# Three-layer transformer kernel: combination sums read back from DRAM, merging sums on VectorE, gate rows loaded a tile ahead, short head products in other PSUM banks

## The chip, the cores and the metric

The kernel runs on one core of a Trainium2 chip. The time is the device time of one execution in microseconds; less is better. All data are fp32, and each product of two fp32 matrices is made of three passes on TensorE (PE): every operand is split into a high half, rounded to the format that PE reads at full speed (`h` at the end of a name), and the remainder (`l`), and the passes are high by high, high by low and low by high.

## The reference, cut to what matters

Sequence 512, width 2048. Two attention layers, then one hybrid layer with 16 meta tokens in front of the sequence, then a normalization. The change is in the end of the second attention layer and in the hybrid layer:

```python
def hybrid_layer(x, gain, w_in, pool_w, pool_scale, w_attn_up, w_pool_up, w_out):
    h = rmsnorm_2(x, gain)
    zin = h @ w_in
    q, k, v, g_attn, u, g_pool, m_attn, m_pool = jnp.split(zin, cuts, axis=-1)
    o_attn = stick_breaking_attention(q, k, v).reshape(B, L, SB_WIDTH)   # 8 heads of 128
    o_attn = o_attn * jax.nn.silu(g_attn)
    y_attn = o_attn @ w_attn_up
    pooled = multiscale_pool(u)          # mean of the last 2, 4, 8, 16 tokens, minus the token
    mixed = jnp.einsum('blgc,gcd->blgd', pooled, pool_w).reshape(B, L, POOL_WIDTH)
    o_pool = mixed * pool_scale * jax.nn.silu(g_pool)
    y_pool = o_pool @ w_pool_up
    merged = jax.nn.sigmoid(m_attn) * y_attn + jax.nn.sigmoid(m_pool) * y_pool
    return x + merged @ w_out

def stick_breaking_block(q_blk, k_pre, v_pre, q0):
    z = scaled scores of the block with its causal keys
    log_1m_beta = where(causal, log_sigmoid(-z), 0)
    between = cumsum(log_1m_beta, reverse=True) - log_1m_beta
    a = where(causal, exp(log_sigmoid(z) + between), 0)
    return a @ v_pre
```

## The kernel before

Activations stand transposed: a tile holds 128 features by 512 tokens (528 with the meta tokens), and 16 such tiles are the width of 2048. A product of the plain kind takes 24 PE passes of 512 columns per weight tile of 128 by 1024 (eight blocks, three passes each). Other products are done in pairs of token halves and feature halves, as in a fast matrix multiplication with fewer products; for these, `t_set` (line 327) forms combinations of two activation tiles: GpSimd adds the high and low halves of both back together (`ra`, `rb`), VectorE forms four sums of halves (`t12`, `t34`), and these are split again (`t12h`, `t12l`, `t34h`, `t34l`).

Weights come by the queue of SyncE (SP) in the order of use into three buffers (`wr`); ScalarE rounds them to `wh`, VectorE subtracts to get `wl`. Some weights are first summed in DRAM by GpSimd's queue (`wsd`). A load of a weight waits until the `wl` three weights before it is done. All other tiles live in 76 equal slots. PSUM has two groups of four banks: `ps_mm` for the large products and `ps_at` for the heads.

The order of PE's instructions is written out by the program: a main sequence of products (`SEQ2`), and generators beside it that are stepped on a clock of emitted work. `start_side(g, delay)` starts one so many units later, and `yield n` in it waits for n units; a unit is about a nanosecond of PE's work. The orders of the other engines are made by a scheduler. The sequence of the hybrid layer is: projections in pairs (with the four pool products `pw` between them), gate products `gp` and `ga`, `pu` (up projection of the pooled part, into `yp`), `au` (up projection of the attention, merged with `yp` into `mg`), and the output.

Beside it run `t_build` (line 1183), which makes the combinations of the normalized input `X2` during the `gp` products, later those of `mg`; `pool_diff` (line 1165), which forms window mean minus token (`pd`) and splits it for `pw`; and `sb_head` for each of the 8 heads. A head takes `v` to `vt` (transposed, then split into `vh`, `vl`), the scores to `zA`, `zB`, `zC`, a softplus of these on ScalarE (`sp`, split to `sph`, `spl`), sums over blocks on GpSimd (`suf`, split to `sufh`, `sufl`), and then adds to the scores the products with a triangle of ones (`tri`). The short products `zm` and `rm` are the parts of the meta tokens, `so` is the head's output. `vt`, `zm`, `rm` and `so` all take their bank from `ps_at`.

The loads for `pu` (`ol`, the pooled part, line 1199) and for `au` (`sgl`, the gate; `ypl`, the result of `pu`) are issued on ScalarE's queue at the place where the tile is emitted. GpSimd adds `ypl` to the gated product (line 1235) and multiplies all gates (line 445).

Of the kernel before, what the change touches and what calls it, by code (L numbers as in the profile page):

```python
# [18 lines left out]
P = 128  # L19
# [85 lines left out]
def trunk_kernel(ctx, tc, xT, w_in, w_qkv, w_out, w_in2, w_pool, w_aup, w_pup, w_out2, metaT, vec, cst, outT):  # L105
# [9 lines left out]
    def slot(name, dt=F32, cols=S):  # L115
        t = slots.tile([P, W], dt, tag="s", name=name)
        return t[:, :cols]
# [7 lines left out]
    def f32(t):  # L125
        return t.bitcast(F32)
# [200 lines left out]
    def t_set(a, b, rb=None):  # L327


        w = a[0].shape[1]  # L330
        n = w // 2
        lo, hi = slice(0, n), slice(n, w)
        ra = slot("ra", F32, w)
        nc.gpsimd.tensor_tensor(ra, f32(a[0]), f32(a[1]), ALU.add)
        if rb is None:
            rb = slot("rb", F32, w)
            nc.gpsimd.tensor_tensor(rb, f32(b[0]), f32(b[1]), ALU.add)
        t12, t34 = slot("t12", F32, w), slot("t34", F32, w)
        tt(t12[:, lo], ra[:, lo], ra[:, hi], ALU.subtract)
        tt(t34[:, lo], ra[:, hi], rb[:, hi], ALU.subtract)  # L340
        tt(t12[:, hi], rb[:, hi], t12[:, lo], ALU.add)
        tt(t34[:, hi], rb[:, lo], t12[:, hi], ALU.subtract)
        p12, p34 = split(t12, "t12", w), split(t34, "t34", w)

        def cut(p, sl):
            return p[0][:, sl], p[1][:, sl]

        return {"t1": cut(p12, lo), "t2": cut(p12, hi), "t3": cut(p34, lo), "t4": cut(p34, hi),
                "b11": cut(a, lo), "b21": cut(b, lo), "b22": cut(b, hi)}
# [88 lines left out]
    def gate_silu(ps, r, name):  # L438
        g = slot(name + "g")
        tt(g, ps, r, ALU.mult)  # L440
        return silu(g, name)

    def silu(g, name):
        a = gate_sigmoid(g, name)
        nc.gpsimd.tensor_tensor(g, g, a, ALU.mult)
        return g
# [14 lines left out]

    xd = [tc.dram_tile([P, NC, S], F32, name=f"xd{i}") for i in range(2)]
# [325 lines left out]
    def layer(lay, h, rd, x_src, x_dst):  # L788
# [68 lines left out]
        for j in range(NC):  # L857
# [11 lines left out]
            else:  # L869
# [5 lines left out]
                lo = slot("Xl", F32R, W)  # L875
                nc.scalar.mul(real(hi), halves(xg), g2)
# [118 lines left out]
    def sb_head(hd):  # L995
# [51 lines left out]
        pm = ps_at("zm")  # L1047
# [19 lines left out]
        pm = ps_at("rm")  # L1067
# [11 lines left out]
        o = ps_at("so")  # L1079
# [13 lines left out]
    def v_split(vf):  # L1093
        tp = ps_at("vt")
        for j in range(NB):
            transp(tp[:, j * P:(j + 1) * P], vf[:, token(j):token(j) + P])
        return split(tp, "v")
# [5 lines left out]
    gad = tc.dram_tile([P, SB, S], F32, name="gad")  # L1103
    gpd = tc.dram_tile([P, 8, S], F32, name="gpd")
# [60 lines left out]
    def pool_diff(cur, uf, w, res, i):  # L1165
        yield 15000
        d = slot("pd")
        ins = nc.vector.scalar_tensor_tensor(d, cur[:, NM:], 1.0 / w, uf[:, NM:], ALU.mult, ALU.subtract)
        behind_pe(ins)
        res[i] = split(d, "pd")  # L1170
# [12 lines left out]
    def t_build(get, upto):  # L1183
        while len(tset) < upto:
            n = len(tset)
            tset.append(t_set(get(n), get(n + 8)))
            yield 8000
# [7 lines left out]

    def o_load(c):
        op[c] = split(load(opd[:, c, :], "ol", queue=nc.scalar), f"o{c}")

    start_side(t_build(x2, 8), 9000)
    for kind, i in SEQ2:  # L1200
# [25 lines left out]
        elif kind == "au":  # L1226
# [4 lines left out]
            ga = load(sgd[:, i, :], "sgl", queue=nc.scalar)  # L1231
            yp = load(ypd[:, i, :], "ypl", queue=nc.scalar)
            ya = slot("ym")
            tt(ya, run_gemm(1, 8, lambda c: oa[c]), ga, ALU.mult)
            nc.gpsimd.tensor_tensor(ya, ya, yp, ALU.add)  # L1235
            mg[i] = split(ya, f"mg{i}")
            if 8 <= i < 8 + EARLYT:
                tset.append(t_set(mg[i - 8], mg[i], ya))
        elif kind == "gp" and i < GPLAIN:
# [3 lines left out]
            nc.gpsimd.dma_start(gpd[:, i, :], gate_silu(ps, sr, "gp"))  # L1243
# [61 lines left out]
    start_side(t_build(mget, 8))  # L1305
# [165 lines left out]
```

## Time and profile before

| | |
|---|---|
| median of 3 runs | 2718.32 us (2716.43 to 2720.26) |
| profiled execution | 2721.86 us |
| its span | 2720.1 us |
| mean granted clock of TensorE | 0.986 |
| PE busy | 97% |
| DVE (VectorE), ACT (ScalarE), POOL (GpSimd) busy | 67%, 48%, 22% |

The span is the time from the first to the last instruction of the profiled execution; a start or a duration below is in microseconds from its beginning. An engine's busy time leaves out the issuing of transfers. The granted clock is the share of TensorE's full speed (2.4 GHz) that it was given; the lower of its two levels is half of that. A wait is put down to the instruction that released it last.

### The profile page before, as it was taken

The numbers are of one execution on the slowest core, as the hardware profiler recorded it, in microseconds if no ns is written. First come the engines' busy times: TensorE is split into PE (matmuls) and PEld (weight loads), VectorE is DVE, ScalarE is ACT, GpSimd is POOL, SyncE is SP. The second block draws the span as 40 slices with busy tenths as digits, with TensorE's granted clock in tenths as the row PEclk, the third lists the DMA queues.
The fourth block names the chain that finished last, engine by engine and source line by source line (L and its number), as shares of the span: only waits on it lengthen the run. The fifth ranks groups of instructions, "written<-read, shape, count | busy, mean of one in ns | idle before, by whom it ended". The sixth has DMA issues, their size and how long they took to land.

```text
span 2720.1 us, 39186 instructions
## 1 busy us (share of the span) xinstructions
PE 2640.2 (97%) x15169; PEld 2301.7 (85%) x15169; DVE 1832.6 (67%) x2675; ACT 1311.0 (48%) x2160; POOL 601.4 (22%) x553
## 2 busy tenths in 40 slices
PE   8999999999999999999999999999999997999897
PEld 6888888888788888888888899999999986777697
DVE  7767566644476756665587777768777664764787
ACT  5445455532344545553344333336666664632353
POOL 4111132222121113224442122000000131313312
PEclk9999999999999999999999999999999998999999
DMA  5455555577654545457733544555555534364455
GB/s 177 118 142 134 133 138 131 150 223 210 177 147 127 138 128 140 127 162 218 196 108 112 156 152 153 161 157 156 161 157 160 168 128 148 118 218 149 126 184 186
DMA packets 138266, 419.76 MB, mean 154 GB/s; under 512 B 15696, under 2 KB 20176, under 8 KB 138080
## 3 DMA queue, kind: packets, MB, share of 16 engines
q1 hardware_dynamic: 93344, 288.40, 33.6%
q0 software_dynamic: 27312, 97.20, 15.9%
q10 hardware_dynamic: 17424, 31.66, 3.5%
q8 instruction: 119, 1.95, 0.3%
q14 instruction: 67, 0.55, 0.1%
HBM read 375.12 MB, written 119.67 MB: 182 GB/s over the span
## 4 chain that ended last, share of the span: by engine, by line
PE 84%; DVE 6%; DMA 4%; issue 2%; ACT 2%; POOL 2%; SPq 0%; DVEq 0%; ACTq 0%; POOLq 0%
PE mm L160 45%; PE y L160 11%; PE z L160 8%; PE x L160 8%; DMA sgl<-sgd 2%; DVE wl L129 2%; PE msc L160 1%; POOL ym L1235 1%; PE qn L160 1%; PE sc L160 1%; PE mo L160 1%; PE o L160 1%; PE tp L164 1%; PE kn L160 1%; DMA ol<-opd 1%
## 5 line engine op out<-in xcount | busy, mean ns | idle before, releaser
L249 ACT CAST wh<-wr 128x1024 fp32r<-128x1024 f32 (+2 forms) x448 | 461.8, 1031 | 647.6 <-PE mm L160 327.3
L129 DVE TENSOR_TENSOR wl<-wr,wh 128x1024 fp32r<-128x1024 f32 (+2 forms) x448 | 575.6, 1288 | 241.1 <-ACT wh L249 227.5
L160 PE MATMUL mm<-hh,wh 128*128 128x512 f32 x1024 | 411.0, 401 | 6.6 <-ACT wh L249 6.4
L160 PE MATMUL mm<-hh,wl 128*128 128x512 f32 x1024 | 405.1, 396 | 4.3 <-DVE wl L129 4.2
L160 PE MATMUL mm<-hl,wh 128*128 128x512 f32 x1024 | 404.9, 395 | 2.9 <-DVE hl L132 2.9
L227 POOL DMA_DIRECT2D wsd<-in_w_in x128 | 88.3, 690 | 730.9 <-PE mm L160 498.0
L160 PEld LDWEIGHTS mm<-hh,wl 128*128 128x128 f32 x1024 | 193.4, 189 | 50.5 <-DVE wl L129 5.8
L160 PEld LDWEIGHTS mm<-hh,wh 128*128 128x128 f32 x1024 | 193.9, 189 | 42.5 <-ACT wh L249 6.4
L160 PEld LDWEIGHTS mm<-hl,wh 128*128 128x128 f32 x1024 | 193.8, 189 | 40.5 <-DVE hl L132 5.3
L249 ACT CAST wh<-ws 128x1024 fp32r<-128x1024 f32 x111 | 116.4, 1049 | 160.1 <-PE y L160 99.3
L160 PE MATMUL y<-t34h,wl 128*128 128x256 f32 (+1 forms) x592 | 166.9, 282 | 0.0
L160 PE MATMUL y<-t34h,wh 128*128 128x256 f32 (+1 forms) x592 | 166.9, 282 | 0.0
L160 PE MATMUL y<-t34l,wh 128*128 128x256 f32 (+1 forms) x592 | 166.8, 282 | 0.0
L129 DVE TENSOR_TENSOR wl<-ws,wh 128x1024 fp32r<-128x1024 f32 x111 | 138.9, 1251 | 29.0 <-ACT wh L249 26.8
L160 PE MATMUL x<-Xl,wh 128*128 128x256 f32 (+1 forms) x512 | 144.7, 283 | 0.0
L160 PE MATMUL x<-Xh,wl 128*128 128x256 f32 (+1 forms) x512 | 144.5, 282 | 0.0
L160 PE MATMUL x<-Xh,wh 128*128 128x256 f32 (+1 forms) x512 | 144.3, 282 | 0.0
L160 PEld LDWEIGHTS y<-t34h,wl 128*128 128x128 f32 x592 | 111.5, 188 | 0.0
L160 PEld LDWEIGHTS y<-t34h,wh 128*128 128x128 f32 x592 | 111.5, 188 | 0.0
L160 PEld LDWEIGHTS y<-t34l,wh 128*128 128x128 f32 x592 | 111.3, 188 | 0.0
L160 PE MATMUL mm<-Xh,wl 128*128 128x512 f32 x256 | 102.5, 400 | 3.7 <-DVE wl L129 3.7
L160 PE MATMUL mm<-Xh,wh 128*128 128x512 f32 x256 | 103.2, 403 | 0.0
(1036 smaller groups left out, 7170.5 us busy)
## 6 DMA issues: line engine op xcount, KB each, us to landing
wr<-in_w_in SPq DMA_DIRECT2D x256, 512.0 KB, 3.7
wsd<-in_w_in POOLq DMA_DIRECT2D x128, 512.0 KB, 5.3
wr<-in_w_out SPq DMA_DIRECT2D x95, 512.0 KB, 4.5
ws<-wsd SPq DMA_DIRECT2D x37, 512.0 KB, 4.2
wr<-wsd SPq DMA_DIRECT2D x37, 512.0 KB, 4.1
wsd<-in_w_out POOLq DMA_DIRECT2D x20, 512.0 KB, 5.7
xd<-xn SPq DMA_DIRECT2D x32, 256.0 KB, 3.6
sgd<-sga ACTq DMA_DIRECT2D x32, 256.0 KB, 2.2
```

What stands on the lines that cost most here:

```text
L129: nc.vector.tensor_tensor(out, a, b, op)
L160: last_pe[0] = nc.tensor.matmul(out, a, b, start=start, stop=stop, skip_group_check=True).ins
L164: nc.tensor.transpose(out, x, ident)
L227: behind_pe(nc.gpsimd.dma_start(dst, src, **kw))
L249: nc.scalar.copy(hi, raw)
L1235: nc.gpsimd.tensor_tensor(ya, ya, yp, ALU.add)
```

## The change

- At the end of layer 1, each normalized tile is also written, unsplit, to DRAM (`xrd`). `t_set` takes `ra` and `rb` as arguments, and `t_build` loads them (`tr`) on SP's queue one step ahead, so that GpSimd's sums go away. Its first delay goes from 9000 to 6000 units with a yield of 3000 after the first loads.
- The merged tiles are written to DRAM (`mgd`) on ScalarE's queue, except the four whose combinations are made at once; `t_build` and the four early `t_set` read them back.
- The gate products of `gp` and the sums of `au` go from GpSimd to VectorE. Those of `ga` stay.
- `vt`, `zm`, `rm` and `so` take their banks from `ps_mm`.
- `pool_diff` starts 9000 units after its window sums in place of 15000.
- `sgl` and `ypl` for `au` are loaded on SP's queue, issued one tile ahead; `ol` is loaded on SP's queue. The `sgl` of `pu` stays on ScalarE's.

```diff
-    def t_set(a, b, rb=None):
+    def t_set(a, b, ra, rb):
...
-        ra = slot("ra", F32, w)
-        nc.gpsimd.tensor_tensor(ra, f32(a[0]), f32(a[1]), ALU.add)
-        if rb is None:
-            rb = slot("rb", F32, w)
-            nc.gpsimd.tensor_tensor(rb, f32(b[0]), f32(b[1]), ALU.add)
...
-    def silu(g, name):
+    def silu(g, name, eng=nc.gpsimd):
         a = gate_sigmoid(g, name)
-        nc.gpsimd.tensor_tensor(g, g, a, ALU.mult)
+        eng.tensor_tensor(g, g, a, ALU.mult)
...
+                xr = slot("xr", F32, W)
+                nc.scalar.mul(real(xr), halves(xg), g2)
+                nc.scalar.mul(halves(xr)[:, :, :M2], halves(metas[:, j * NM:(j + 1) * NM]), g2)
+                nc.scalar.dma_start(xrd[:, j, :], xr)
...
-        pm = ps_at("zm")
+        pm = ps_mm("zm")
...
-        pm = ps_at("rm")
+        pm = ps_mm("rm")
...
-        o = ps_at("so")
+        o = ps_mm("so")
...
-        tp = ps_at("vt")
+        tp = ps_mm("vt")
...
     def pool_diff(cur, uf, w, res, i):
-        yield 15000
+        yield 9000
...
-    def t_build(get, upto):
-        while len(tset) < upto:
+    def t_build(get, raw, w):
+
+        ahead = {}
+
+        def fetch(n):
+            if n < 8:
+                ahead[n] = [load(raw[:, c, :], "tr", w) for c in (n, n + 8)]
+
+        fetch(len(tset))
+        yield 3000
+        while len(tset) < 8:
             n = len(tset)
-            tset.append(t_set(get(n), get(n + 8)))
+            fetch(n + 1)
+            tset.append(t_set(get(n), get(n + 8), *ahead.pop(n)))
             yield 8000
...
+    def au_loads(i):
+        return load(sgd[:, i, :], "sgl"), load(ypd[:, i, :], "ypl")
+
     def o_load(c):
-        op[c] = split(load(opd[:, c, :], "ol", queue=nc.scalar), f"o{c}")
-
-    start_side(t_build(x2, 8), 9000)
+        op[c] = split(load(opd[:, c, :], "ol"), f"o{c}")
+
+    start_side(t_build(x2, xrd, W), 6000)
...
-            ga = load(sgd[:, i, :], "sgl", queue=nc.scalar)
-            yp = load(ypd[:, i, :], "ypl", queue=nc.scalar)
+                ahead = {0: au_loads(0)}
+            if i + 1 < NC:
+                ahead[i + 1] = au_loads(i + 1)
+            ga, yp = ahead.pop(i)
             ya = slot("ym")
             tt(ya, run_gemm(1, 8, lambda c: oa[c]), ga, ALU.mult)
-            nc.gpsimd.tensor_tensor(ya, ya, yp, ALU.add)
+            tt(ya, ya, yp, ALU.add)
+            if i not in range(8, 8 + EARLYT):
+                nc.scalar.dma_start(mgd[:, i, :], ya)
             mg[i] = split(ya, f"mg{i}")
             if 8 <= i < 8 + EARLYT:
-                tset.append(t_set(mg[i - 8], mg[i], ya))
+                tset.append(t_set(mg[i - 8], mg[i], load(mgd[:, i - 8, :], "tr"), ya))
...
-            nc.gpsimd.dma_start(gpd[:, i, :], gate_silu(ps, sr, "gp"))
+            nc.gpsimd.dma_start(gpd[:, i, :], gate_silu(ps, sr, "gp", nc.vector))
...
-    start_side(t_build(mget, 8))
+    start_side(t_build(mget, mgd, S))
```

The order of PE's instructions is the same in both kernels, row by row. On the other engines it moves. VectorE's order around the third pool product, where `pd` and `pdl` are the two differences and their low halves, `ab` and `c` are sums of the paired products, and `ws` is the sum of two weights; before:

```order
L129 TENSOR_TENSOR ab<-y,m_13817 128x264
L129 TENSOR_TENSOR wl<-wr,wh 128x512
L1168 SCALAR_TENSOR_TENSOR pd<-pl,uf 128x512
L129 TENSOR_TENSOR wl<-ws,wh 128x1024
L129 TENSOR_TENSOR pdl<-pd,pdh 128x512
L1168 SCALAR_TENSOR_TENSOR pd<-pl,uf 128x512
L129 TENSOR_TENSOR ws<-ws,wr 128x1024
L129 TENSOR_TENSOR wl<-wr,wh 128x1024
L129 TENSOR_TENSOR pdl<-pd,pdh 128x512
```

and after:

```order
L129 TENSOR_TENSOR ab<-m_13883,y 128x264
L129 TENSOR_TENSOR wl<-ws,wh 128x1024
L1169 SCALAR_TENSOR_TENSOR pd<-pl,uf 128x512
L129 TENSOR_TENSOR pdl<-pd,pdh 128x512
L1169 SCALAR_TENSOR_TENSOR pd<-pl,uf 128x512
L129 TENSOR_TENSOR wl<-wr,wh 128x1024
L129 TENSOR_TENSOR pdl<-pd,pdh 128x512
L129 TENSOR_TENSOR ab<-y,m_13883 128x264
L129 TENSOR_TENSOR wl<-wr,wh 128x512
```

Both pairs stand ahead of the sum `ab` of `y` and of the 512-column weight (that of `pw` itself), where before they stood behind these.

ScalarE's order at the first head that starts in the last gate tile, where `o0h` to `o3h` are the high halves of the pooled part, `gaa` belongs to the gate and `sp` is the head's softplus; before:

```order
L151 CAST o0h<-ol 128x512
L136 ACTIVATE gaa<-gaa 128x512
L1180 DMA ol<-opd 128x512
L249 CAST wh<-wr 128x1024
L151 CAST o1h<-ol 128x512
L1180 DMA ol<-opd 128x512
L151 CAST o2h<-ol 128x512
L1180 DMA ol<-opd 128x512
L151 CAST o3h<-ol 128x512
L151 CAST vh<-vt 128x512
L136 ACTIVATE sp<-zA 128x512
```

and after:

```order
L151 CAST o0h<-ol 128x512
L136 ACTIVATE gaa<-gaa 128x512
L151 CAST o1h<-ol 128x512
L249 CAST wh<-wr 128x1024
L151 CAST o2h<-ol 128x512
L249 CAST wh<-wr 128x1024
L151 CAST o3h<-ol 128x512
L151 CAST vh<-vt 128x512
L136 ACTIVATE sp<-zA 128x512
```

The loads are gone from this engine, and a second weight's high half stands ahead of `o3h`. The loads are in SP's order after, among the weights of `pu`:

```order
L194 DMA wr<-in_w_pup 128x1024 x3
L1181 DMA ol<-opd 128x512
L194 DMA wr<-in_w_pup 128x1024
L1181 DMA ol<-opd 128x512 x2
L194 DMA wr<-in_w_pup 128x1024
L1181 DMA ol<-opd 128x512
L194 DMA wr<-in_w_pup 128x1024
L1181 DMA ol<-opd 128x512 x4
```

The fourth `ol` stands behind the fifth weight of `pu`, and the last four stand together behind the sixth.

## Rows read from the trace of the kernel before

**Rows 1.** The page's first part: busy time of each engine, its share of the span, and the number of its instructions.

```profile
PE 2640.2 (97%) x15169; PEld 2301.7 (85%) x15169; DVE 1832.6 (67%) x2675; ACT 1311.0 (48%) x2160; POOL 601.4 (22%) x553
```

**Rows 2.** The waits of TensorE (PE) over the whole span: what waited for what, microseconds in total, how many times, and the longest.

```profile
PE mm L160 <- DVE wl L129: 15.0, 7, 4.2
...
PE pw L160 <- DVE pdl L129: 5.4, 4, 1.4
PE mm L160 <- DVE ym L129: 4.9, 3, 2.8
PE pw L160 <- ACT pdh L151: 3.5, 4, 0.9
...
PE mm L160 <- ACT o5h L151: 2.5, 1, 2.5
```

**Rows 3.** Busy time by stretch. The columns are the stretch, its length, then the busy time and the number of instructions of PE, PEld, DVE, ACT and POOL, PE's granted clock as a share of full speed, the share of the DMA engines' time, and GB/s.

```profile
1400.00:1460.00 60.00, 56.34 (x235) 44.64 (x234) 56.70 (x62) 31.10 (x47) 27.07 (x24) 0.97 0.33 106
1500.00:1560.00 60.00, 55.89 (x438) 53.95 (x436) 44.29 (x52) 23.72 (x31) 8.83 (x8) 1.00 0.49 152
1560.00:1660.00 100.00, 95.21 (x705) 91.41 (x706) 76.01 (x89) 37.97 (x51) 30.00 (x24) 0.95 0.47 153
...
2250.00:2290.00 40.00, 25.18 (x83) 17.75 (x83) 19.47 (x28) 19.99 (x36) 6.13 (x8) 0.74 0.32 92
...
2300.00:2410.00 110.00, 104.53 (x496) 86.66 (x495) 73.20 (x119) 66.07 (x122) 27.18 (x40) 0.97 0.49 159
...
2480.00:2510.00 30.00, 27.61 (x112) 21.68 (x111) 18.71 (x29) 10.57 (x15) 10.28 (x6) 0.94 0.47 143
2510.00:2555.00 45.00, 37.86 (x157) 28.63 (x155) 25.13 (x28) 11.69 (x16) 21.82 (x13) 1.00 0.42 130
2555.00:2580.00 25.00, 20.80 (x89) 16.97 (x89) 22.42 (x31) 11.94 (x17) 6.11 (x6) 0.86 0.36 117
```

**Rows 4.** The `xo` stage of layer 1. First the stretch, with columns as in rows 3, then the group of ScalarE's instructions there that scale a tile: line, engine, operation, names, shapes and count, then busy time and mean ns of one, then idle time before them.

```profile
1205.00:1375.00 170.00, 170.00 (x736) 137.79 (x735) 97.60 (x102) 65.87 (x101) 66.87 (x49) 1.00 0.71 200
...
L876 ACT ACTIVATE Xh<-xg,vecs 128x512 fp32r<-128x512 f32 x16 | 11.4, 710 | 0.0
```

**Rows 5.** Groups of instructions of VectorE (DVE) and of GpSimd (POOL) from 1400 to 1460 us, columns as in the second of rows 4.

```profile
L129 DVE TENSOR_TENSOR t34l<-t,t34h 128x528 fp32r<-128x528 f32 x7 | 17.7, 2533 | 0.5 <-ACT t34h L151 0.5
L129 DVE TENSOR_TENSOR wl<-wr,wh 128x1024 fp32r<-128x1024 f32 x9 | 15.3, 1697 | 0.0
...
L334 POOL TENSOR_TENSOR ra<-Xh,Xl 128x528 f32<-128x528 f32 x6 | 8.0, 1338 | 0.1
L445 POOL TENSOR_TENSOR gpg<-gpg,gpa 128x512 f32<-128x512 f32 x6 | 7.9, 1324 | 42.2 <-ACT gpa L136 42.2
```

**Rows 6.** VectorE's timeline in the gate stage: start, duration, engine, line, operation, tiles, and in brackets the idle time before it with what ended it.

```profile
1430.27 6.14 DVE L129 TENSOR_TENSOR t34l<-t,t34h 128x528 fp32r<-128x528 f32 x1
...
1436.68 1.21 DVE L129 TENSOR_TENSOR wl<-wr,wh 128x1024 fp32r<-128x1024 f32 x1
...
1439.96 0.70 DVE L129 TENSOR_TENSOR t34l<-t,t34h 128x528 fp32r<-128x528 f32 x1
```

**Rows 7.** The timelines around the third of the four pool products, columns as in rows 6: the second split difference on VectorE, the products on PE that wait for its two halves, and GpSimd's last window sum ahead of it.

```profile
1607.65 0.68 DVE L129 TENSOR_TENSOR pdl<-pd,pdh 128x512 fp32r<-128x512 f32 x1
...
1606.53 0.50 PE L160 MATMUL pw<-pdh,wh 128*128 128x512 f32 x1 [0.88 <-ACT pdh L151]
1608.38 0.69 PE L160 MATMUL pw<-pdl,wh 128*128 128x512 f32 x1 [1.35 <-DVE pdl L129]
...
1590.69 3.92 POOL L1160 TENSOR_TENSOR pl<-pl 128x525 f32<-128x525 f32 x2
```

**Rows 8.** PE's timeline at the first head that starts in the last gate tile, columns as in rows 6.

```profile
2249.51 0.39 PE L160 MATMUL mm<-Xl,wh 128*128 128x512 f32 x1
2249.74 0.39 PE L160 MATMUL mm<-Xh,wl 128*128 128x512 f32 x1
2259.76 0.76 PE L160 MATMUL zm<-qh,zwh 128*128 128x512 f32 x1 [9.63 <-DVE vl L129]
...
2269.39 0.40 PE L160 MATMUL zA<-sph,tri 128*128 128x512 f32 x1
```

**Rows 9.** ScalarE's timeline (ACT) in the same place: the last half that it reads for the products of `pu` before the head, the head's first softplus step, and the last of its three sum halves.

```profile
2257.68 0.62 ACT L151 CAST o3h<-ol 128x512 fp32r<-128x512 f32 x1 [4.30 <-DMA ol<-opd]
...
2258.68 0.60 ACT L136 ACTIVATE sp<-zA 128x512 f32<-128x512 f32 x1
...
2268.28 0.62 ACT L151 CAST sufh<-suf 128x512 fp32r<-128x512 f32 x1 [1.16 <-POOL suf L1038]
```

**Rows 10.** One tile of the merging products, `mg11`, on three engines, columns as in rows 6; ACTq is ScalarE's instruction queue as it issues a transfer.

```profile
2508.11 0.33 ACTq L1180 DMA_DIRECT2D sgl<-sgd  x1
...
2514.00 0.62 ACT L151 CAST mg11h<-ym 128x512 fp32r<-128x512 f32 x1 [3.90 <-POOL ym L1235]
...
2511.00 0.69 DVE L129 TENSOR_TENSOR ym<-mm,sgl 128x512 f32<-128x512 f32 x1 [1.41 <-DMA sgl<-sgd]
...
2511.83 2.14 POOL L1235 TENSOR_TENSOR ym<-ym,ypl 128x512 f32<-128x512 f32 x1 [5.77 <-DVE ym L129]
```

**Rows 11.** The transfers issued from 2500 to 2545 us: what, from which engine's queue, how many, their size, and the median time from issue to landing.

```profile
wr<-in_w_out SPq DMA_DIRECT2D x8, 512.0 KB, 3.7
sgl<-sgd ACTq DMA_DIRECT2D x5, 256.0 KB, 3.7
```

More of the change, by code (lines that the diff above doesn't have):

```diff
@@ L436, in gate_sigmoid, with gate_silu @@
         return a
-    def gate_silu(ps, r, name):
+    def gate_silu(ps, r, name, eng=nc.gpsimd):
         g = slot(name + "g")
         tt(g, ps, r, ALU.mult)
-        return silu(g, name)
-    def silu(g, name):
+        return silu(g, name, eng)
+    def silu(g, name, eng=nc.gpsimd):
         a = gate_sigmoid(g, name)
-        nc.gpsimd.tensor_tensor(g, g, a, ALU.mult)
+        eng.tensor_tensor(g, g, a, ALU.mult)
         return g
@@ L460, in load_consts1 @@
         nc.sync.dma_start(diag_t, cst[:, C_DIAG:C_DIAG + S])
+    xrd = tc.dram_tile([P, NC, W], F32, name="xrd")
     xd = [tc.dram_tile([P, NC, S], F32, name=f"xd{i}") for i in range(2)]
@@ L1103, in trunk_kernel @@
     gad = tc.dram_tile([P, SB, S], F32, name="gad")
+    mgd = tc.dram_tile([P, NC, S], F32, name="mgd")
     gpd = tc.dram_tile([P, 8, S], F32, name="gpd")
```

## The prediction

> **What bounds the kernel now.** I read the page's first part, then the waits of TensorE, then a table by stretch, and in each stretch that loses time the timeline of the engine waited for. TensorE is busy for 2640.2 us of the span [rows 1], so nothing but its lost time can be won: at most 79.9 us of idling, and what a lowered clock adds. Its order of instructions is the same in both kernels, so the question is only how long it waits at each place. The waits name the places [rows 2, 8]: late weight halves, one product `zm` (9.6 us), the pool product `pw` (5.4 + 3.5 us), the gated sums `ym`, and the halves of `o`. The stretches [rows 3] give each place its size. I count as lost what the stretch is longer than PE's busy time, and its length times one minus the granted clock; a lowered clock inside an idle stretch is counted twice by this, so the sizes are upper bounds.
>
> - A, gate stage `gp`, 1400 to 1460: 3.7 + 1.8 = 5.5 us
> - B, the four `pw`, 1500 to 1660: 4.1 + 4.8 + 5.0 = 13.9 us
> - C, first head after the last gate tile, 2250 to 2290: 14.8 + 10.4 = 25.2 us
> - D, the heads inside `pu`, 2300 to 2410: 5.5 + 3.3 = 8.8 us
> - G, first `au` tiles, 2480 to 2510: 2.4 + 1.8 = 4.2 us
> - F, later `au` tiles and the start of the output, 2510 to 2580: 7.1 + 4.2 + 3.5 = 14.8 us
>
> Together 72.4 us. Elsewhere the change touches stretches in which PE does not wait.
>
> **The change, part by part.**
>
> *Unsplit tiles written out.* In the `xo` stage ScalarE gets 16 scalings at the 0.71 us of those it has already, 16 small ones of 16 columns that cannot take longer, and issues 16 writes: 11 to 23 us, in a stretch of 170 us in which ScalarE is busy for 65.9 [rows 4]. So I price it at nothing; without that cover it would cost those 11 to 23 us. The writes are 4.3 MB, 25 GB/s on top of 200 at a DMA share of 0.71 [rows 4]: about 0.80, still below full.
>
> *A: sums off GpSimd.* In 1400 to 1460 VectorE is busy for 56.7 of 60 us [rows 3], but much of this is not work: `t34l` takes 2533 ns on average, `wl` 1697 [rows 5], while a `t34l` that no GpSimd operation overlaps takes 0.70 us and one beside GpSimd's sums took 6.14 [rows 6]. GpSimd ran `ra`, `rb` and the gate products at 1.3 us each [rows 5]. With these gone VectorE gets back 7 x (2.53 - 0.70) = 12.8 us from `t34l` and 9 x (1.70 - 1.21) = 4.4 from `wl`, and takes six gate products at the 0.69 us of a 512-column product [rows 10], 4.1 us. It then has some 13 us of slack in 60. The `tr` tiles come by SP a step ahead. Gain 5 of 5.5 us; if a `tr` lands late, 3.
>
> *B: `pool_diff` earlier.* The second `pdl` of a group ended at 1608.33, and PE waited 0.88 and then 1.35 us for the pair [rows 7]. In the order after, both `pd` and `pdl` stand two products ahead, before the last `ab` and before the next group's weight sum. the delay is 6000 units, some 6 us, shorter, so the second `pdl` would end at about 1602. GpSimd's last sum for this group ended at 1594.6 [rows 7]; two differences and two splits at 0.69 us and ScalarE's two rounds fit between, with a microsecond or two to spare or to wait for. A wait of that size would hold up the weight halves behind it, which an interval of one product (5.6 us) covers. Gain 12 of 13.9; if half of the wait comes back, 7.
>
> *C: banks and `o` loads.* PE stood 9.6 us at `zm` for the bank of `vt`, which `vl` had to read [rows 8]. In the new banks `zm` need not wait. But what follows does not come earlier. ScalarE read `o3h` at 2257.68 after 4.3 us of waiting, and the softplus came behind it at 2258.68; the last `sufh` ended at 2268.9 [rows 9]. In the order after, a `wh` stands before `o3h` that needs the end of the gate product PE then runs; from 2249.97 that is about 28 matmuls of 512 columns at the 0.23 us of their starts [rows 8], 2256.4. With `wh`, `o3h` and `vh` behind it, softplus starts at about 2258.6, where it started before, and `o3` itself cannot land much sooner, since its load stands on SP behind a weight. So PE reaches the triangle product at about 2258 and waits there until 2269, where it began it before (2269.39 [rows 8]). The stall moves; the saving is 0.5 us, and the low clock behind a stall stays. What does go is the wait for `o4h` to `o7h`: 2.5 us at `o5h` [rows 2] and, with the other three and the low clock, 5 to 6. Their four loads now stand together on SP and land before ScalarE comes to them. I take 6 us of the 25.2; 3 if one load stays late, 8 if the clock recovers sooner.
>
> *D: other heads.* `rm` and `zA` wait for a bank that `vl` holds; those banks change owner. As in C a wait can move to the next product that needs ScalarE's result. Bounds are 0 and 8 us; I take 4, half.
>
> *G and F: `au`.* Before, the gate `sgl` was issued by ScalarE at 2508.11, as late as ScalarE got to it in its order; VectorE had `ym` from PE but started at 2511.00, GpSimd's sum took 2.14 us more, and `mg11h` started at 2514.00 [rows 10]. In the order after the two loads of a tile stand a whole tile ahead of use (5.57 us: 24 passes of 0.23 us [rows 8]), plus the weight loads between. A load takes about 3.7 us [rows 11]. So `ym` starts as soon as PE is done, the sum takes VectorE 0.69 instead of 2.14 us, and the banks come free 3 to 4 us sooner, more than the 2.8 us of PE's longest wait there. New work on VectorE is 16 x 0.69 = 11 us over 90. G gains 3 of 4.2 (0 to 4), F 11 of 14.8 (5 to 14): what stays is a weight half late behind `t_set`.
>
> Sum: 5 + 12 + 6 + 4 + 3 + 11 = 41 us. The profiled execution took 2721.86 us, 1.8 us around its span; that is 3.5 above the median of 2718.32. 2718.3 - 41 = **2677 us**. The lower bounds add up to 3 + 7 + 3 + 0 + 0 + 5 = 18 us (2700), the upper to 5.5 + 13.9 + 8 + 8 + 4 + 14 = 53 (2665).
>
> A rule speaks against part of this. The Trainium skill ("Trainium Kernel Development and Optimization", Key Constraints) says that transfers from the queues of SP, ScalarE and GpSimd share the same 16 engines, and that several issuers save issue time alone. By it, taking `sgl`, `ypl` and `ol` from ScalarE's queue to SP's brings nothing by itself and costs SP the issuing; only their earlier place can help. The rows allow that: `sgl` and the weights on two queues land after the same median of 3.7 us [rows 11]. This is the first rival.
>
> **The rivals.**
>
> 1. *The loads are no earlier in effect.* SP issues in order, and a load waits there for a free slot and behind a weight load that waits for a `wl`. If the `au` loads leave only when the tile before is done, G and F stay but for GpSimd's shorter sum (2 us of 19), C's loads bring 3 and D nothing: 5 + 12 + 3 + 0 + 2 = 22 us, **2696**. For it: slots are 76 for everything, and VectorE does wait for transfers now. Against: on SP each pair stands one tile ahead in the order. Chance 0.22.
> 2. *All stalls but the moved one go*, the clock recovers with them: 53 to 58 us, **2662**. For it: VectorE would have slack at each place. Against: each shortened wait so far ends on another engine 1 to 2 us later. Chance 0.15.
> 3. *Slower: SP blocks.* Twenty-eight `tr` loads, 32 `au` loads and 8 `ol` loads now stand among the weights. Where one waits for a slot or for its tile's write to DRAM, all weights behind it wait. There are three buffers, so PE is two products (11 us) ahead at most, and copy and split take 2.3 us of these: from a block of about 8 us on, each microsecond is PE's. If 28 steps each block 3 us too long, 84 us are lost against 41 won: **2761**. For it: `mgd` is read back within the last tiles. Against: `xrd` is written some tens of microseconds before it is read. It decides from 1.5 us a step. Chance 0.05.
> 4. *No change*: VectorE takes over 17 us of products and sums and loses at its own places what it wins, **2718**. Against: it wins 17 us in A alone. Chance 0.05.
>
> My forecast has 0.53.
>
> **The numbers.** The likeliest case gives 2677, by its own bounds 2665 to 2700. For 8 in 10 the range takes in most of rivals 1 and 2: 2660 to 2704. Three repeats of this kernel span 0.14%, so 0.2% (5.4 us) is about what a measurement can tell from no change. Faster by more: 0.53 + 0.22 + 0.15 - 0.02 for tails = 0.88; within: 0.06; slower: 0.06.
>
> **What would show it.** A: `t34l` back at 0.7 us and no wait for `wl` in the gate stage. B: no `pw` waiting for `pdh` or `pdl`, clock near 1. C: no wait at `zm`, but about 10 us at the first triangle product behind `sufh`, and `o4h` to `o7h` without a wait. D: the waits at `rm` and `zA` smaller. G and F: VectorE's `ym` waits for PE and no longer for `sgl`. The forecast is wrong if PE waits for `wl` while SP stands at a load of another kind (rival 3), if `ym` still waits for `sgl` (rival 1), or if the triangle starts well before 2269 less what was won ahead of it (rival 2).

## The result, and the profile after

The changed kernel takes **2674.97 us** (median of 4, 2674.15 to 2675.18) against 2718.86 us for the kernel before on the same chip: a ratio of 0.9843, 95% interval 0.9831 to 0.9856, so 1.6% faster (the medians lie 43.9 us apart). The forecast was 2677, with a range of 2660 to 2704. The profiled execution took 2675.18 us at a mean granted clock of 0.992.

The page's first part and TensorE's waits after, which answer to [rows 1] and [rows 2]; columns as there:

```profile
PE 2622.8 (98%) x15169; PEld 2296.0 (86%) x15169; DVE 1804.9 (68%) x2699; ACT 1323.7 (50%) x2192; POOL 513.5 (19%) x501
```

```profile
PE mm L160 <- ACT wh L249: 7.6, 2, 6.6
PE mm L160 <- DVE wl L129: 5.0, 3, 3.2
...
PE mm L160 <- DVE ym L129: 4.1, 1, 4.1
...
PE zA L160 <- DVE ql L132: 2.4, 2, 1.9
```

PE idles 50.6 us of its span of 2673.4 in place of 79.9. Every wait at `pw`, at `zm` and at `o5h` to `o7h` is gone, and late `wl` cost 5.0 us in place of 15.0: the 10 us that went are those of A, G and F, and none is left in the six stretches. (The 7.6 at `wh`, and what is left at `wl`, lie at the start of the program but for a microsecond each at the end; they are not this change's.) What is new are two waits at `zA`, for `sph` and `sufh`, 7.6 us together (their lines stand at e9); and the three waits for `ym`, 4.9 us, have become one of 4.1.

By stretch, with the columns of [rows 3]; each stretch is cut about where the same work stands, so it is shorter than its fellow there (in order: A, the two of B, C, D, G, then F in two):

```profile
1400.00:1454.00 54.00, 54.00 (x234) 43.58 (x233) 40.06 (x68) 32.09 (x47) 3.37 (x6) 1.00 0.52 176
1494.00:1549.00 55.00, 55.00 (x439) 54.34 (x438) 45.09 (x56) 23.68 (x31) 9.41 (x9) 1.00 0.55 169
1549.00:1639.00 90.00, 89.95 (x708) 88.35 (x708) 74.27 (x84) 38.48 (x52) 29.56 (x23) 1.00 0.50 161
2229.00:2262.00 33.00, 23.86 (x86) 17.68 (x85) 18.75 (x28) 19.02 (x35) 5.45 (x8) 0.79 0.30 99
2271.00:2376.00 105.00, 101.69 (x500) 85.06 (x499) 73.31 (x121) 65.92 (x122) 28.10 (x40) 1.00 0.52 169
2445.00:2471.00 26.00, 26.00 (x114) 21.15 (x113) 16.08 (x25) 9.41 (x13) 0.00 (x0) 1.00 0.48 156
2471.00:2514.00 43.00, 38.90 (x158) 31.16 (x157) 29.88 (x49) 13.96 (x20) 0.00 (x0) 0.92 0.66 220
2514.00:2533.00 19.00, 19.00 (x95) 15.92 (x94) 12.31 (x16) 8.99 (x12) 4.36 (x5) 1.00 0.47 159
```

A, B and G run without a gap at the full clock. C still loses 9.1 us and a clock of 0.79, D 3.3 us, and the first part of F, the `au` tiles, 4.1 us and a clock of 0.92. The second part of F, the start of the output, loses nothing, where before it lost 4.2 us at a clock of 0.86.

Because PE's order is the same in both kernels, the start of one and the same PE instruction can be compared between two traces, and its shift says what was won up to there. So the trace shows what each term of the sum came to. The table holds all kernels of this study (microseconds won against the trace of before; places as in the prediction, but F is taken on to 2600 us of before, so that the output's first pair is in it; "rest" is everything outside them):

| kernel | A | B | C | D | G | F | rest | all |
|---|---|---|---|---|---|---|---|---|
| forecast | 5 | 12 | 6 | 4 | 3 | 11 | 0 | 41 |
| changed kernel | 6.0 | 15.2 | 7.6 | 6.1 | 4.6 | 9.1 | -2.0 | 46.6 |
| e1, `pool_diff` alone | 0.0 | 15.4 | 2.1 | -0.1 | 3.2 | -0.8 | 0.4 | 20.1 |
| e2, gates alone | 4.5 | 0.1 | 1.1 | 1.6 | 1.2 | -1.7 | -1.7 | 5.1 |
| e3, gates back | 6.0 | 15.1 | 6.0 | -0.1 | 4.6 | 10.1 | 0.2 | 41.9 |
| e4, banks back | 6.0 | 15.2 | 8.4 | -1.5 | 4.6 | 10.3 | -0.6 | 42.5 |
| e5, `ol` on ScalarE's queue | 6.0 | 15.2 | 0.6 | 4.4 | 4.5 | 9.0 | 1.8 | 41.5 |
| e6, `au` loads on ScalarE's, ahead | 6.0 | 15.0 | 6.2 | 4.2 | 4.6 | 16.1 | -0.2 | 51.9 |
| e7, `au` loads on SP, not ahead | 6.0 | 15.2 | 6.1 | 4.2 | 4.6 | 2.9 | 1.7 | 40.8 |
| e8, sum of `au` on GpSimd | 6.0 | 15.2 | 6.0 | 4.7 | 4.6 | 10.2 | -0.6 | 46.2 |
| e9, split of `o` later | 6.0 | 15.2 | 14.9 | 4.7 | 4.6 | 8.7 | 2.1 | 56.3 |
| e10, three early `t_set` | 6.0 | 15.2 | 7.5 | 1.7 | 4.6 | 9.5 | 3.6 | 48.1 |
| e11, e9 and e10 | 6.0 | 15.2 | 14.4 | 5.6 | 4.6 | 9.1 | 2.0 | 57.0 |
| e12, e9 and e6 | 6.0 | 15.2 | 14.6 | 5.7 | 4.6 | 16.0 | 2.1 | 64.2 |

A and B repeat to 0.2 us from kernel to kernel wherever the code there is the same; C moves by 1.6 (6.0 to 7.6 among the changed kernel, e3, e6, e7, e8 and e10, which have the same code there), F by 1.6 (8.7 to 10.3), and D by 6 (-0.1 in e3 to 6.1). A microsecond or two is not read at C and F, and at D only the waits are: there the clock of kernels that are alike lies between 0.95 (e3) and 1.00 (the changed kernel). The last column belongs to single executions; the verdicts below go by the medians.

### The profile page after: what moved, and what is told of

Same layout as the page of the kernel before. It is cut to its first block, busy times and chain, and to the rows that moved or that the text cites. A ratio compares the mean times of both kernels' runs of the same rounds, so it can differ in the third digit from the quotient of the medians.

```text
span 2673.4 us, 39297 instructions
## 1 busy us (share of the span) xinstructions
PE 2622.8 (98%) x15169; PEld 2296.0 (86%) x15169; DVE 1804.9 (68%) x2699; ACT 1323.7 (50%) x2192; POOL 513.5 (19%) x501
## 4 chain that ended last, share of the span: by engine, by line
PE 92%; DVE 3%; DMA 2%; ACT 1%; issue 1%; POOL 1%; ACTq 0%; SPq 0%; DVEq 0%; POOLq 0%
PE mm L160 52%; PE y L160 12%; PE x L160 8%; PE z L160 8%; PE msc L160 1%; PE qn L160 1%; PE sc L160 1%; PE mo L160 1%; PE o L160 1%; PE tp L164 1%; PE kn L160 1%; PE v L160 1%; PE mtp L164 1%; DVE wl L129 1%; PE qr L160 1%
## 5 line engine op out<-in xcount | busy, mean ns | idle before, releaser
L129 DVE TENSOR_TENSOR wl<-wr,wh 128x1024 fp32r<-128x1024 f32 (+2 forms) x448 | 568.3, 1272 | 247.5 <-ACT wh L249 234.2
```

The lines of the kernel that those rows point to most:

```text
L129: nc.vector.tensor_tensor(out, a, b, op)
```

## The experiments

### e1: the pool differences alone

```diff
 # the kernel before
-        yield 15000
+        yield 9000
```

> The kernel before with one edit: pool_diff starts after 9000 units in place of 15000. My theory: the place of the differences in the order is all of term B, so the four products pw wait for neither pdh nor pdl, and the pool stretch is 15 us shorter: about 2704 us. Rival: term B came from the relief of GpSimd and VectorE (sums and gate products moved), and with these in place the window sums or the weight halves are late instead: some wait at pw or at a weight half stays, less than 7 us saved, 2712 us or more.

Measured: 2699.55 us, ratio 0.993 (0.9907 to 0.9953), by its theory (2704) and a little better. The pool stretch of this kernel, columns as in [rows 3]:

```profile
1500.00:1645.00 145.00, 144.93 (x1147) 142.67 (x1146) 119.40 (x139) 62.06 (x83) 38.86 (x32) 1.00 0.53 165
```

PE idles 0.07 us in 145, at full clock, and no wait at `pw` is left. 15.4 us were won there, as much as in the changed kernel: term B is the place of the differences in the order, and neither the sums nor the gates have a part in it. The 3.2 us at G are the wait for a `wl` that stands there before, only shorter (1.0 us for 2.1) with less of the low clock behind it; why this edit shortens it, no run shows.

### e2 and e3: which GpSimd work held VectorE up in the gate stage

```diff
 # e2, the kernel before (the call; gate_silu and silu take the engine)
-            nc.gpsimd.dma_start(gpd[:, i, :], gate_silu(ps, sr, "gp"))
+            nc.gpsimd.dma_start(gpd[:, i, :], gate_silu(ps, sr, "gp", nc.vector))
 # e3, the changed kernel
-            nc.gpsimd.dma_start(gpd[:, i, :], gate_silu(ps, sr, "gp", nc.vector))
+            nc.gpsimd.dma_start(gpd[:, i, :], gate_silu(ps, sr, "gp"))
```

> The kernel before with one edit: the gate products of gp run on VectorE, the sums ra and rb stay on GpSimd. My theory: VectorE gets back about a third of the 17 us that GpSimd costs it there and pays 4 to 5.5 us for the products, so the gate stage still waits for weight halves: 0 to 2 us saved, 2717 us. Rival: the products were what made VectorE late, the stall of 6 us goes, 2713 us.

> The changed kernel with one part undone: the gate products of gp on GpSimd again, the sums read back from DRAM as in the change. My theory: taking the sums off GpSimd is what frees VectorE, so the gate stage still loses nothing: 2675 us, within 1. Rival: both had to go, the stage loses up to 6 us again, 2681 us.

Measured: e2 2715.05 us, ratio 0.9991 (0.9982 to 1.0001), so not told from no change; e3 2675.19, ratio 0.985 (0.9831 to 0.9868), the same as the changed kernel. In the stage itself e2 won 4.5 of the 6.0 us, which I had put at 0 to 2. VectorE's groups there in e2, columns as in [rows 5]:

```profile
L129 DVE TENSOR_TENSOR t34l<-t,t34h 128x528 fp32r<-128x528 f32 x7 | 16.0, 2291 | 0.0
L129 DVE TENSOR_TENSOR wl<-wr,wh 128x1024 fp32r<-128x1024 f32 x9 | 15.1, 1681 | 0.1
...
L129 DVE TENSOR_TENSOR t12l<-t,t12h 128x528 fp32r<-128x528 f32 x7 | 4.9, 701 | 0.3 <-ACT t12h L151 0.3
```

`t34l` and `wl` are nearly as slow as before (2291 and 1681 ns for 2533 and 1697), so the big loss of time on VectorE stayed. Only `t12l` came back, from 1090 ns on average before to 701: 2.7 us, with the 1.7 us of `t34l` some 4.4, against 4.1 us of new products. VectorE's balance is near zero, and yet PE's two waits for a `wl` here, 1.7 and 1.9 us before, shrank to one of 0.9. So it isn't VectorE's sum of work alone that sets the stall; which weight half comes late, and behind what, counts too, and that I did not take apart further. In e3 the sums are gone:

```profile
L129 DVE TENSOR_TENSOR wl<-wr,wh 128x1024 fp32r<-128x1024 f32 x9 | 11.0, 1217 | 0.6 <-ACT wh L249 0.6
L129 DVE TENSOR_TENSOR t34l<-t,t34h 128x528 fp32r<-128x528 f32 x7 | 7.1, 1014 | 0.9 <-ACT t34h L151 0.8
```

Here `t34l` is down to 1014 ns and `wl` to 1217, and the stage loses nothing, with the gate products still on GpSimd. Taking the sums off is enough, as my theory had it; moving the gates alone won 4.5 of the 6.0 us too, which it had not.

### e4 and e5: banks and loads at the heads

```diff
 # e4, the changed kernel; the same for rm, so and vt
-        pm = ps_mm("zm")
+        pm = ps_at("zm")
 # e5, the changed kernel
-        op[c] = split(load(opd[:, c, :], "ol"), f"o{c}")
+        op[c] = split(load(opd[:, c, :], "ol", queue=nc.scalar), f"o{c}")
```

> The changed kernel with one part undone: zm, rm, so and vt take their banks from the group of the heads again. My theory: at the head of the last gate tile the wait of 9 to 10 us stands before zm again and the one of 7.6 us at the triangle goes, so this place loses 1 to 3 us; the later heads lose the 6 us that they won: 2682 us. Rival: the banks made all of the 7.6 us won at the first place too, 2689 us.

> The changed kernel with one part undone: the eight loads ol are issued on ScalarE's queue again. My theory: o4 to o7 are late again as they were before, and the place of the last gate tile loses 5 to 6 us: 2680 us. Rival: these waits went because the head's chain ends earlier in the new banks, no loss, 2675 us.

Measured: e4 2678.37 us (ratio 0.9859, 0.9843 to 0.9876), 3.4 above the changed kernel where its theory had 7; e5 2680.12 (0.986, 0.9845 to 0.9875), by its theory. TensorE's waits in e4 and then in e5, and the issue of the last `ol`: of the last four on SP's queue in the changed kernel, of the very last on ScalarE's in e5:

```profile
PE zm L160 <- DVE vl L129: 8.6, 1, 8.6
...
PE rm L160 <- DVE vl L129: 2.4, 1, 2.4
PE zA L160 <- DVE vl L129: 1.7, 1, 1.7
```

```profile
PE mm L160 <- ACT o5h L151: 2.2, 1, 2.2
```

```profile
2238.05 1.74 SPq L1181 DMA_DIRECT2D ol<-opd  x4
```

```profile
2256.44 0.33 ACTq L1181 DMA_DIRECT2D ol<-opd  x1
```

With the banks back the 8.6 us at `zm` stand there again, and yet place C won 8.4 us, no less than with the new banks: `zm`'s new bank won nothing at C, the stall only stands later. At D the waits for `vl` are back (4.1 us at `rm` and `zA`), which the new banks had taken away, and its gain with them (-1.5). The waits are the banks'; how much of the time is theirs can't be read closely, since e3, with the new banks, won nothing at D either: the clock there was 0.95 in both, 1.00 in the changed kernel. At that one clock the banks are worth 1.4 us (-0.1 against -1.5). With the loads on ScalarE's queue C falls to 0.6 from the 6 to 7.6 of its equals and the waits for `o5h` to `o7h` return. On that queue the last four loads were issued one by one as ScalarE came through its order, each beside the split of the tile before, from 2246.25 to 2256.44; on SP all four were issued by 2239.8, eleven microseconds before ScalarE read the first of them. So nearly all that was won at C are the `ol` loads (e1 and e2, with no edit there, show 2.1 and 1.1).

### e6, e7 and e8: what `au` owes to which part

```diff
 # e6, the changed kernel
-        return load(sgd[:, i, :], "sgl"), load(ypd[:, i, :], "ypl")
+        return load(sgd[:, i, :], "sgl", queue=nc.scalar), load(ypd[:, i, :], "ypl", queue=nc.scalar)
 # e7, the changed kernel
-                ahead = {0: au_loads(0)}
-            if i + 1 < NC:
-                ahead[i + 1] = au_loads(i + 1)
-            ga, yp = ahead.pop(i)
+            ga, yp = au_loads(i)
 # e8, the changed kernel
-            tt(ya, ya, yp, ALU.add)
+            nc.gpsimd.tensor_tensor(ya, ya, yp, ALU.add)
```

> The changed kernel with one part undone: sgl and ypl of au are issued on ScalarE's queue, still one tile ahead in the program. My theory, which goes by the earlier place: 2675 us, within 2. Rival: the gain came from leaving ScalarE's in-order queue, where a load stands behind a weight half that waits for PE; the au stretches lose part of the 13 us that they won, 2680 us or more.

> The changed kernel with one part undone: sgl and ypl of au are loaded on SP's queue, but at the tile that uses them, not one ahead. My theory: the place is what counts, so these stretches lose most of the 13 us that they won: 2684 us or more. Rival: on SP a load is issued in front of weights that are fetched two products ahead, so it is early anyway: 2675 us, within 2.

> The changed kernel with one part undone: the sum of the gated product and ypl runs on GpSimd again, 2.1 us in place of 0.69. My theory: the bank is free once VectorE has multiplied, and the split after it has time, so PE loses 1 to 3 us: 2677 us. Rival: the longer chain to mg and GpSimd's share of VectorE's time bring back 5 us or more: 2680 us.

Measured: e6 **2667.34 us** (0.9813, 0.9798 to 0.9828), faster than the changed kernel; e7 2681.09 (0.9865, 0.9846 to 0.9883), between its theory (2684 or more) and its rival (2675); e8 2674.72 (0.9842, 0.9828 to 0.9857), not told from the changed kernel.

Where F was won shows when it is split by the same table (microseconds won; the `au` tiles up to 2545.9 us of before, the halves of the last tile with the first weight of the output to 2554.7, the late `wl` there to 2580, the output's first pair to 2600):

| kernel | `au` tiles | last tile | late `wl` | first pair | F |
|---|---|---|---|---|---|
| changed kernel | -1.1 | 2.9 | 6.8 | 0.4 | 9.1 |
| e6 | 5.9 | 2.9 | 6.8 | 0.4 | 16.1 |
| e7 | -2.4 | 2.9 | 6.8 | -4.5 | 2.9 |
| e8 | 0.0 | 2.9 | 6.8 | 0.4 | 10.2 |
| e10 | 5.9 | 3.0 | 6.9 | -6.2 | 9.5 |
| e1, e2 | -1.1, -1.0 | 0.3, 0.4 | 0.5, 0.9 | -0.5, -2.0 | -0.8, -1.7 |

The largest part is not at `au` but at the late `wl` behind it. The kernel before there, VectorE, GpSimd and PE, then VectorE in the changed kernel:

```profile
2556.10 1.74 DVE L129 TENSOR_TENSOR t34l<-t,t34h 128x512 fp32r<-128x512 f32 x1
...
2558.11 1.21 DVE L129 TENSOR_TENSOR wl<-wr,wh 128x1024 fp32r<-128x1024 f32 x1
```

```profile
2545.20 1.27 POOL L334 TENSOR_TENSOR ra<-mg4h,mg4l 128x512 f32<-128x512 f32 x1
...
2555.59 1.71 POOL L337 TENSOR_TENSOR rb<-mg15h,mg15l 128x512 f32<-128x512 f32 x1
```

```profile
2559.37 0.80 PE L160 MATMUL mm<-mg8h,wl 128*128 128x512 f32 x1 [4.20 <-DVE wl L129]
```

```profile
2504.78 0.68 DVE L129 TENSOR_TENSOR t34l<-t,t34h 128x512 fp32r<-128x512 f32 x1
```

Eight sums `ra` and `rb` of the merged tiles follow each other on GpSimd, VectorE's operations beside them take 1.0 to 1.1 us longer each (`t34l` 1.74 us in place of 0.68), and the weight half behind them is 4.2 us late. The changed kernel reads these sums back from DRAM, and neither the slow operations nor the wait is there. So this is the mechanism of A once more. The traces show it; no run leaves the merged sums alone on GpSimd.

TensorE's waits in e7:

```profile
PE mm L160 <- DVE ym L129: 6.4, 2, 3.5
...
PE x L160 <- ACT m L365: 3.0, 1, 3.0
```

Of the 6.2 us by which e7 stays behind the changed kernel at F, 4.9 lie behind `au`, at the output's first pair: ScalarE's order there holds two weight halves ahead of the copies `m` that PE's `x` waits for, where the changed kernel has the copies first. One tile ahead on SP is worth only what is lost in the `au` tiles, 1 to 2.5 us (-2.4 against -1.4 to 0.1 in kernels that are alike there). Moving the sum to VectorE is worth nothing (e8): on GpSimd it took 1.29 us there, not the 2.14 of before, the bank is free once VectorE's product has read it, and the split has time.

G is 4.6 in all three. Its stall before was a `wl` behind a `ym` that waited for its gate:

```profile
2492.59 0.69 DVE L129 TENSOR_TENSOR ym<-mm,sgl 128x512 f32<-128x512 f32 x1 [1.53 <-DMA sgl<-sgd]
2493.20 1.22 DVE L129 TENSOR_TENSOR wl<-wr,wh 128x1024 fp32r<-128x1024 f32 x1
```

```profile
2494.47 0.50 PE L160 MATMUL mm<-oa0h,wl 128*128 128x512 f32 x1 [2.12 <-DVE wl L129]
```

e6 puts back the queue alone and e7 the place alone, and in both the gate is there early enough; a kernel with both put back was not run.

e6 fell on neither side that I had named: the queue matters, but the other way. In the changed kernel VectorE and PE stand so at the end of `au`:

```profile
2440.38 0.69 DVE L129 TENSOR_TENSOR ym<-mm,sgl 128x512 f32<-128x512 f32 x1 [2.37 <-PE mm L160]
...
2471.32 0.68 DVE L129 TENSOR_TENSOR ym<-mm,sgl 128x512 f32<-128x512 f32 x1
...
2474.51 1.23 DVE L129 TENSOR_TENSOR wl<-wr,wh 128x1024 fp32r<-128x1024 f32 x1 [1.78 <-ACT wh L249]
...
2480.05 1.23 DVE L129 TENSOR_TENSOR wl<-wr,wh 128x1024 fp32r<-128x1024 f32 x1 [2.24 <-ACT wh L249]
...
2482.39 0.68 DVE L129 TENSOR_TENSOR ym<-mm,sgl 128x512 f32<-128x512 f32 x1
```

```profile
2483.22 0.77 PE L160 MATMUL mm<-mg0h,wh 128*128 128x512 f32 x1 [4.11 <-DVE ym L129]
```

The first row is a tile before the early combinations: `ym` waits for PE. In the four tiles with a `t_set` the order made for VectorE holds two `wl` for each `ym`, and a `wl` cannot start until PE frees a buffer, so VectorE falls behind by one tile in each (the two `ym` shown are 11 us apart, and PE's tile is 5.6). `ym` of the thirteenth tile starts at 2482.39, and PE, which needs the bank, waits until 2483.22. In e6 the order has one `mg` half ahead of a `wl` instead of behind it and other small swaps. VectorE and then PE there:

```profile
2479.94 0.68 DVE L129 TENSOR_TENSOR ym<-mm,sgl 128x512 f32<-128x512 f32 x1
...
2482.05 0.40 PE L160 MATMUL mm<-mg0h,wh 128*128 128x512 f32 x1
```

`ym` is done 1.4 us before PE comes, without a wait, and the low clock behind the stall is spared too: 7 us (5.9 for -1.1 in the `au` tiles). The edit is to the queue; what it changed is the order in which the scheduler placed VectorE's rows.

### e9 to e12: on from there

In the changed kernel ScalarE's order at place C is what holds the head up (its timeline, then PE's):

```profile
2235.21 1.05 ACT L249 CAST wh<-wr 128x1024 fp32r<-128x1024 f32 x1 [4.71 <-PE mm L160]
2236.18 0.62 ACT L151 CAST o3h<-ol 128x512 fp32r<-128x512 f32 x1
2236.71 0.58 ACT L151 CAST vh<-vt 128x512 fp32r<-128x512 f32 x1
2237.19 0.60 ACT L136 ACTIVATE sp<-zA 128x512 f32<-128x512 f32 x1
```

```profile
2241.26 0.79 PE L160 MATMUL zA<-sph,tri 128*128 128x512 f32 x1 [4.46 <-ACT sph L151]
...
2245.96 0.69 PE L160 MATMUL zA<-sufh,none 128*128 128x384 f32 x1 [3.18 <-ACT sufh L151]
```

The second `wh` waits for PE until 2235.2, and `o3h`, `vh` and the softplus stand behind it.

```diff
 # e9, the changed kernel
             if i == SB - 1:
-                for c in range(PRE):
-                    o_load(c)
+                raws = [load(opd[:, c, :], "ol") for c in range(PRE)]
             nc.gpsimd.dma_start(gad[:, i, :], gate_silu(run_gemm(2, 8, x2), sr, "ga"))
             if i == SB - 1:
                 X2 = None
+                for c in range(PRE):
+                    op[c] = split(raws[c], f"o{c}")
+                raws = None
 # e10, the changed kernel
-EARLYT = 4
+EARLYT = 3
```

> The changed kernel with one edit: the first four ol are loaded at the same place, but split into halves only after the last gate product is emitted, so that vh and the head's softplus stand ahead of them and of the second weight half in ScalarE's order. My theory: the stall of 7.6 us at the triangle product is ScalarE's order and nothing else, it goes, with the low clock behind it: 2666 us. Rival: the chain of the head itself takes as long, or o0h to o7h are late in its place: 2673 us or more.

> The changed kernel with one edit: three of the combinations of the merged tiles are made in the au stage, not four. My theory: the last wait of PE there (4.1 us for ym, which VectorE reads behind t12l and t34l of the fourth) goes: 2671 us. Rival: the fifth combination left for later makes the first pair of the output wait: 2675 us or more.

> The changed kernel with the edits of the two runs before together. My theory: they lie in different places and add up: 2662 us. Rival: one gives back what the other won, because weights and splits then come at other times: 2668 us or more.

Measured: e9 **2666.52 us** (0.9814, 0.9799 to 0.983), e10 2673.93 (0.984, 0.9826 to 0.9854), e11 2666.75 (0.9815, 0.9801 to 0.9829). In e9 the wait at the triangle is gone, and one before `o0h` has come in its place; in e10 the wait for `ym` is gone, and the first pair of the output waits for the combination left for later:

```profile
PE mm L160 <- ACT o0h L151: 4.7, 1, 4.7
```

```profile
PE z L160 <- ACT t12h L151: 4.0, 1, 4.0
```

So e9 went by my theory (7.3 us at C; the median is 8 us lower), though part of the stall, 4.7 us, only moved to `o0h`, and e10 by its rival: one wait changed for another. e11 is no better than e9, where its theory had 2662: what e10 wins in the `au` tiles it gives back at the output's first pair.

> The changed kernel with two edits together: the first four ol are split only after the last gate product, as in the run that did this alone, and sgl and ypl of au are issued on ScalarE's queue, one tile ahead, as in the run that did that alone. My theory: the two lie in different places, 7.3 us at the head of the last gate tile and 7 us at the end of au, and add up: 2660 us, within 2. Rival: the second gain was a chance of the order that the scheduler made, and with the first edit the order falls out otherwise: 2666 us.

Measured: **2658.26 us** (0.9787, 0.9774 to 0.98), 58 us below the kernel before on the same chip; beside the changed kernel's 0.9843 that is half a per cent more, and by its theory (2660, within 2). Both gains are there in full (14.6 at C, 16.0 at F).

## Why the prediction was right, point by point

**What bounds it, and the accounting.** Right: nearly all was won in the six stretches named, out of PE's idling and the clock behind it. The sum came to 41 us; the profiled executions lie 46.7 apart and the medians 43.9. That the total is so near is in part luck: A, B, C, D and G brought 9.5 us more than forecast, F 1.9 and the rest 2.0 less, and F's term is right in size by another mechanism than its own (below). Nor are the sizes upper bounds, as was said of them: A won 6.0 of 5.5, B 15.2 of 13.9 and G 4.6 of 4.2.

**Unsplit tiles written out.** Right, hidden. The `xo` stage after, columns as in [rows 4]:

```profile
1205.00:1375.00 170.00, 170.00 (x735) 137.81 (x734) 88.21 (x102) 78.46 (x132) 64.87 (x49) 1.00 0.79 223
```

PE is busy for all of it, ScalarE took 12.6 us more, and the DMA share is 0.79 (0.80 estimated).

**A.** Right in its end (6.0 for 5), and in the price of VectorE's operations, whose groups after answer to [rows 5]:

```profile
L129 DVE TENSOR_TENSOR wl<-wr,wh 128x1024 fp32r<-128x1024 f32 x9 | 11.0, 1221 | 1.9 <-ACT wh L249 1.9
...
L129 DVE TENSOR_TENSOR t34l<-t,t34h 128x528 fp32r<-128x528 f32 x7 | 4.9, 700 | 0.1
```

`t34l` takes 700 ns, `wl` 1221, and VectorE is busy for 40 of 54 us. (The forecast's own figures leave 16 us of slack in 60, not 13: 3.3 + 12.8 + 4.4 - 4.1; nothing hangs on it.) The step that was wrong is to go by VectorE's sum of work alone: e2 leaves that nearly as it was and still wins 4.5 us.

**B.** Right in its mechanism, mis-sized: 15.2 for 12. The second `pdl` of the third group and the products that were late in [rows 7], VectorE and then PE:

```profile
1586.53 0.69 DVE L129 TENSOR_TENSOR pdl<-pd,pdh 128x512 fp32r<-128x512 f32 x1
```

```profile
1592.83 0.39 PE L160 MATMUL pw<-pdl,wh 128*128 128x512 f32 x1
```

The half ends at 1587.2, more than 5 us ahead of its product at 1592.8. The reserve for half of the wait to come back wasn't needed: GpSimd's window sum had that margin.

**C.** Right in size, and in the step that the stall moves: e4 shows that the banks won nothing there, e5 that the loads won nearly all. Softplus started behind the second `wh`, `o3h` and `vh`, as was worked out. A smaller step was off: I had one wait until the last `sufh`, but the triangle's first product needs `sph` only, so PE worked a little between two waits, and they cost 7.6 us where 11 were forecast.

**D.** Right in sign, sized by half of a bound: 6.1 for 4, though kernels that are equal there lie between -0.1 and 6.1. The waits for `vl` are gone, and come back with the banks (e4); 1.9 and 0.5 us for `ql` came up in their place, so that part of the stall moved, as was left possible. PE's waits there went from 5.4 to 3.4 us in all; the other 4 us are the clock, 1.00 for 0.97, which the change is not shown to cause.

**G.** 4.6 for 3. The gate was late, as the step had it, but what PE waited for was the `wl` behind `ym` on VectorE, not a bank. It takes less than was priced: the gain is the same with the loads not ahead (e7), on ScalarE's queue (e6), and with the sum on GpSimd (e8).

**F.** 9.1 for 11, near by luck: the step was wrong. The forecast gave the gain to the `au` loads and the shorter sum, and let a weight half late behind `t_set` stay. It is that half which went, 6.8 us with the clock behind it, because the merged sums left GpSimd, for which F has no term. In the `au` tiles the old waits for `ym` went, but the new one, for a `ym` that stands behind a `wl` on VectorE, cost as much: -1.1 us. What the earlier loads could win there is seen where that wait is not: 5.9 us (e6, e10). The shorter sum was worth nothing (e8). To what the 2.9 us at the last tile are due, no run tells apart.

**The rule on the queues**, from the Trainium skill ("Trainium Kernel Development and Optimization", Key Constraints), that several queues only save issuing: what helped was an earlier issue, as was inferred from it, but e5 shows that the queue itself decides how early that is. With the line of the program unchanged, SP's queue is worth some 5 to 7 us at C. In e6 the queue moved the time by 7 us too, but by the order that the scheduler then gave VectorE, not by the transfers.

**The rivals.** None came. The first would have left G and F; the second needed the moved stall to cost nothing; of the third and the fourth there was no sign, PE waits for no `wl` in any of the six stretches.

## What to carry to other kernels

Where the order of the bound engine is fixed, compare the start of the same instruction in two traces: each edit's share is then read at its place, here to 0.2 us at A and B and to a microsecond or two at C and F, where medians of the whole cannot tell 0.1%. And cut a place finely enough that each wait stands by itself: F as a whole hid that its gain lay behind the tiles for which it was forecast. Before freeing a bank, follow what the freed engine does next: if its next input comes from the same late chain, the stall only stands later, and what helps is to take the row in front of that chain (here a weight's half and four splits) out of its way. And after any edit look at the order made for the engines beside it: a queue chosen for a load can win or lose more by the rows it shifts than by the load.

## What the runs showed of the hardware

An operation of VectorE on two SBUF tiles can be held through a whole run of GpSimd operations, not only for one of them. In e2 (as in [rows 6] of before) VectorE, then GpSimd:

```profile
1426.36 6.09 DVE L129 TENSOR_TENSOR t34l<-t,t34h 128x528 fp32r<-128x528 f32 x1
...
1426.71 1.34 POOL L334 TENSOR_TENSOR ra<-Xh,Xl 128x528 f32<-128x528 f32 x1
...
1430.54 1.34 POOL L337 TENSOR_TENSOR rb<-Xh,Xl 128x528 f32<-128x528 f32 x1
```

The `t34l` that takes 0.70 us alone took 6.09 us, from before the first of four sums that follow each other within 0.1 us until 0.6 us after the last. Where GpSimd ran single gate products of 1.3 us (e3), `t34l` took 1.01 us on average. The Trainium skill ("SBUF — State Buffer", SBUF: two separate sides) tells of a port pair that one engine locks for an instruction while the other blocks; the trace agrees with the blocking, and shows in addition that VectorE did not get in between four instructions that followed each other. It need not be so: at the start of the output before, beside eight sums in a row, each operation of VectorE took only 1.0 to 1.1 us longer (lines at e6 to e8), so it did get in between. What makes the difference, no run here shows. In these traces a GpSimd operation that stood alone cost VectorE a fraction of a microsecond on average, and a run of two to eight sums 3 to 8 us.
